# One float32 stream on SyncE's queue and one bf16 stream on GpSimd's, and the negated mean made by ScalarE, in a masked-patch loss kernel

## The chip, the cores and the metric

The kernel runs on one core of one Trainium2 chip. The metric is the device time of one execution in microseconds (us), as the median of several executions. A lower time is better.

## The reference

There are 32 images of 147 masked patches (75% of 196), each patch a row of 768 float32 numbers. `pred` and `target` both have the shape 32 x 147 x 768. Each row of the target is normalised by its own mean and variance, the squared distance to the predicted row is averaged over the row, and the row averages are averaged for each image:

```python
mean = target.mean(axis=-1, keepdims=True)
var = target.var(axis=-1, keepdims=True)
target = (target - mean) / np.sqrt(var + 1e-6)
loss = np.mean((pred - target) ** 2, axis=-1)
return loss.mean(axis=-1).astype(np.float32)
```

Both inputs together are 28.9 MB, all of which is read once; 32 numbers are written.

## The kernel before, in words

**Tiling.** Four partitions belong to each image, so 32 images fill 128 partitions. Each partition holds 37 rows of 768 numbers, called columns here and numbered 0 to 36; the last column of every fourth partition would lie outside the image, so the one with number 36 (called `REST`, line `REST = KM`) is loaded for 96 partitions alone. A column of 128 rows is 0.393 MB of float32 in memory. A "piece" is one DMA of up to four neighbouring columns, in which each partition receives one contiguous run (12 KB of source for four columns, 3 KB for one).

**Streams.** Pieces of the target are named t with their first column (t0, t4, ...), those of the prediction p. Before the change, t36 and t0 are loaded as float32 by SyncE's queue, and all 22 others by GpSimd's queue, which converts them to bf16 on the way. Their order is written out in the list `stream`: targets run about eight columns ahead of predictions, and it ends with t32-33, p24-27, t34-35, p28-29, p30-31, p32-33, p34, p35. At most eight pieces of GpSimd's queue are in flight: each issue from the ninth on waits on GpSimd for the landing of the piece eight places earlier.

**Stages of the work**, each by columns:

- `stats(g)` for a group g of columns: VectorE takes two `bn_stats` for each column (line 140) and one `bn_aggr` (line 141), which gives mean and variance (`mv`). Then, once for the group, ScalarE takes the square root of variance plus eps (line 142), VectorE takes the reciprocal `r` (line 143) and makes `nmr` = -mean * r (line 144). Groups have four columns, and two at the end.
- `normalise` on GpSimd (line 158): s = t * r + nmr for each column, written as bf16.
- `subtract` on TensorE (line 178) for a unit of two columns (one, for the last two units, 34 and 35, and for `REST`): three matmuls with minus the identity on s, then three with the identity on p, added up in a PSUM tile `z`. There are two `z` tiles, so a unit's first matmul waits until ScalarE has squared the unit two places earlier.
- `square` on ScalarE (line 184): z squared, summed along the row into a column of `rl`.
- `sums` on TensorE (line 190): a matmul with a mask adds up the four partitions of each image. At the end VectorE reduces 15 columns (line 224) and SyncE stores 32 numbers (line 225).

**Order.** Every engine works its own instructions strictly as they are listed. The list is made when the program is built: each step is given a due time by `at(when, step)` from simple planning costs and planned landings, and all steps are sorted by it. On ScalarE the small square roots of `stats` and the long squares stand in one sequence; likewise GpSimd holds both `normalise` and the issues of its DMAs. Near the end, ScalarE's sequence before the change is: square of unit 22 (columns 22 and 23), square of unit 24, square root of columns 34-35, then the squares of units 26, 28, 30, 32, 34 and 35.

Of the kernel before, what the change touches and what calls it, by code (L numbers as in the profile page):

```python
# [7 lines left out]
F32 = mybir.dt.float32  # L8
BF16 = mybir.dt.bfloat16
ALU = mybir.AluOpType  # L10
ACTF = mybir.ActivationFunctionType
# [3 lines left out]
def kernel(  # L15
# [19 lines left out]
    REST = KM  # L35
# [21 lines left out]
    for c in range(12, KM - 4, 4):  # L57
        stream += [("t", c, c + 4, "sw"), ("p", c - 8, c - 4, "sw")]
    stream += [("t", KM - 4, KM - 2, "sw"), ("p", KM - 12, KM - 8, "sw"), ("t", KM - 2, KM, "sw"),
               ("p", KM - 8, KM - 6, "sw"), ("p", KM - 6, KM - 4, "sw"), ("p", KM - 4, KM - 2, "sw"),  # L60
               ("p", KM - 2, KM - 1, "sw"), ("p", KM - 1, KM, "sw")]
# [7 lines left out]
    land, issue = {}, []  # L69
    t = 2.7  # L70
    for kind, c0, c1, q in stream:
        t += (c1 - c0) * D * 4 * rows_of(c0) / 430e3
        issue.append(t + 1.0)
        for c in range(c0, c1):
            land[kind, c] = t + 1.0
# [8 lines left out]
    def load(kind, c0, c1, q):  # L84
# [8 lines left out]
    lanes = [0.0] * 8  # L93
    k = 0
    for i, piece in enumerate(stream):
        if piece[3] == "hw":
            at(-1.0, lambda piece=piece: load(*piece))
        else:
            at(lanes[k % 8] + (0.01 * k), lambda piece=piece: load(*piece))
            lanes[k % 8] = issue[i] + 0.2  # L100
            k += 1

    ident = singles.tile([P, P], BF16)
    nident = singles.tile([P, P], BF16)
# [20 lines left out]
    def stats(g):  # L125
        n, K = rows_of(g[0]), len(g)
        r = small.tile([P, K], F32, name="r")
        nmr = small.tile([P, K], F32, name="nmr")
        for i, c in enumerate(g):
            rs[c] = (r[:n, i:i + 1], nmr[:n, i:i + 1])  # L130
        if not norm_pix_loss:
            pin(nc.vector.memset(r, 1.0))
            pin(nc.vector.memset(nmr, 0.0))
            return
        mv = small.tile([P, K, 2], F32, name="mv")
        for i, c in enumerate(g):
            til, o = tbuf[c]
            st = small.tile([P, 2, 6], F32, name="st")
            for j in range(2):
                pin(nc.vector.bn_stats(out=st[:n, j, :], in_=til[:n, o + j * half:o + (j + 1) * half]))  # L140
            pin(nc.vector.bn_aggr(out=mv[:n, i], in_=st[:n]))  # L141
        pin(nc.scalar.activation(out=r[:n], in_=mv[:n, :, 1], func=ACTF.Sqrt, bias=eps_t[:n], scale=1.0))  # L142
        pin(nc.vector.reciprocal(out=r[:n], in_=r[:n]))  # L143
        pin(nc.vector.scalar_tensor_tensor(out=nmr[:n], in0=mv[:n, :, 0], scalar=-1.0,  # L144
                                           in1=r[:n], op0=ALU.mult, op1=ALU.mult))


    def normalise(u, i):
        c = u[i]
        n = rows_of(c)  # L150
        if i == 0:
            s = work.tile([P, 2 * D], BF16, name="s")
            for m, cc in enumerate(u):
                sbuf[cc] = (s, m * D)
        s, so = sbuf[c]
        til, o = tbuf[c]
        r, nmr = rs[c]
# [36 lines left out]
    for g in groups:  # L194
        dve = max([dve] + [land["t", c] for c in g])
        at(dve, lambda g=g: stats(g))
        dve += 1.26 * len(g) + 0.8
        for c in g:
            u = next(u for u in units if c in u)
            pool = max(pool, dve + 0.1)  # L200
            at(pool, lambda u=u, i=u.index(c): normalise(u, i))
            pool += 1.1
            ready[c] = pool + 0.1
    free = [0.0, 0.0]
    for u in units:
# [7 lines left out]
        i = main_units.index(u) if u in main_units else -1  # L213
# [47 lines left out]
```

## Time and profile before

| what | value |
|---|---|
| median of 3 runs | 81.1 us (80.77 to 81.3) |
| the profiled execution: its time | 80.73 us |
| the profiled execution: its span, first to last instruction | 79.0 us |
| mean granted TensorE clock | 0.861 |
| busy time: TensorE matmuls, VectorE, ScalarE, GpSimd | 38.7, 45.7, 32.5, 50.1 us |
| `bn_stats` (line 140), one | 533 ns mean, 74 of them |
| `normalise` (line 158), one | 976 ns mean, 37 of them |
| square of two columns (line 184), one | 1431 ns mean, 17 of them |
| square root (line 142), one | 296 ns mean, 12 of them |
| `nmr` (line 144), one | 161 ns mean, 12 of them |
| issue of a target piece on GpSimd (line 89) | 589 ns mean, 9 of them |
| bytes written by DMA, packets | 15.43 MB, 3444 |
| bytes read from memory | 28.90 MB |

The page of a profile has numbered parts: busy times by engine; the span in 40 equal slices, with the busy share of each engine in tenths and the rate of the DMAs in GB/s; the DMA queues; the chain of work that ended last, followed back from the last instruction; and the costliest groups of instructions, with what ended the idle time before them. Beside the page, the trace answers questions: a timeline of instructions in a stretch of time, with the idle time before each and what released it, and the packets and bytes of each DMA queue in a stretch. `<-` in a group or timeline row stands between what is written and what is read. GB/s counts bytes as written, so a piece that is converted to bf16 counts half of what was read for it. One execution is profiled, so durations are of that one.

### The profile page before, as it was taken

Reading aid. Unit: us, or ns where it says so; the run is one execution under the profiler, and the core shown is the slowest. Engines: PE = TensorE matmul, PEld = TensorE weight load, DVE = VectorE, ACT = ScalarE, POOL = GpSimd, SP = SyncE. Lnnn points to the kernel's source line nnn. Section 1 sums busy time; section 2 is a strip of 40 time slices with the busy share of each in tenths; the row PEclk is TensorE's granted clock in tenths of the full one; section 3 lists DMA queues with packets and bytes.
Section 4 is the critical chain, followed back from the end, with each engine's and each line's share of the span. In section 5 each row is a group of like instructions: output and inputs, shape, how many; then the busy total and the mean of one; then the engine's idle time right before and its main releaser. Section 6 shows DMA issues by size and latency. Waiting matters only on the chain.

```text
span 79.0 us, 602 instructions
## 1 busy us (share of the span) xinstructions
PE 38.7 (49%) x126; PEld 13.4 (17%) x126; DVE 45.7 (58%) x137; ACT 32.5 (41%) x53; POOL 50.1 (63%) x73
## 2 busy tenths in 40 slices
PE   0000330008990069985317980991399496496500
PEld 0000210001320023231102320320131031223300
DVE  0061039979799799797797089529779267000000
ACT  5000000050100590872931760583134873999700
POOL 4998802059789899897797795399779360800000
PEclk9999999999999655599965569759956999999996
DMA  0799999999999999999999999999999999990000
GB/s 0 182 412 317 311 218 218 211 218 218 211 215 218 211 216 218 211 211 218 218 211 215 218 215 209 221 215 211 205 227 202 210 210 220 199 165 4 0 0 0
DMA packets 3444, 15.43 MB, mean 195 GB/s; under 512 B 432, under 2 KB 784, under 8 KB 3312
## 3 DMA queue, kind: packets, MB, share of 16 engines
q0 software_dynamic: 3136, 13.52, 84.2%
q1 hardware_dynamic: 304, 1.87, 6.2%
q14 instruction: 3, 0.02, 0.1%
q8 instruction: 1, 0.02, 0.1%
HBM read 28.90 MB, written 0.00 MB: 366 GB/s over the span
## 4 chain that ended last, share of the span: by engine, by line
DMA 42%; DVE 31%; ACT 7%; POOL 5%; PE 4%; issue 4%; SPq 1%; ACTq 0%
DMA p<-in_pred_dram 30%; DVE st L140 23%; DMA t<-in_target_dram 12%; DVE mv L141 5%; ACT z L184 5%; POOL s L158 5%; PE z L178 4%; ACT r L142 2%; DVE r L143 1%; DVE nmr L144 1%; SPq L89 1%; POOL t L89 1%; PE acc L190 0%; DVE ob L224 0%; ACTq L256 0%
## 5 line engine op out<-in xcount | busy, mean ns | idle before, releaser
L140 DVE BATCH_NORM_STATS2 st<-t 128x6 f32<-128x384 bf16 (+2 forms) x74 | 36.3, 533 | 14.4 <-DMA t<-in_target_dram 14.4
L158 POOL TENSOR_SCALAR s<-t,r,nmr 128x768 bf16<-128x768 bf16 (+2 forms) x37 | 35.9, 976 | 13.3 <-DVE nmr L144 13.0
L178 PE MATMUL z<-s,nident 128*128 128x512 bf16 (+3 forms) x57 | 21.4, 492 | 26.6 <-POOL s L158 23.7
L184 ACT ACTIVATE z<-z 128x1536 f32<-128x1536 f32 (+2 forms) x20 | 26.7, 1336 | 2.0 <-PE z L178 2.0
L178 PE MATMUL z<-p,ident 128*128 128x512 bf16 (+3 forms) x57 | 20.6, 478 | 8.9 <-DMA p<-in_pred_dram 8.9
L142 ACT ACTIVATE r<-mv,eps_t 128x4 f32<-128x4 f32 (+2 forms) x12 | 3.6, 296 | 39.4 <-DVE mv L141 39.4
L178 PEld LDWEIGHTS <-nident 128*128 128x128 bf16 (+1 forms) x57 | 5.8, 117 | 39.5 <-ACT z L184 16.3
L89 POOL DMA_DIRECT2D p<-in_pred_dram x13 | 7.7, 594 | 5.2 <-DMA t<-in_target_dram 3.2
L178 PEld LDWEIGHTS <-ident 128*128 128x128 bf16 (+1 forms) x57 | 7.0, 123 | 20.5 <-issue 17.8
L141 DVE BATCH_NORM_AGGREGATE mv<-st 128x2 f32<-128x12 f32 (+1 forms) x37 | 7.7, 208 | 1.3
L89 POOL DMA_DIRECT2D t<-in_target_dram x9 | 5.3, 589 | 0.0
L143 DVE RECIPROCAL r<-r 128x4 f32<-128x4 f32 (+2 forms) x12 | 2.1, 172 | 4.6 <-ACT r L142 4.6
L224 DVE TENSOR_REDUCE ob<-acc 32x1 f32<-32x15 f32 x1 | 0.2, 161 | 7.9 <-PE acc L190 7.9
L184 ACT ACTIVATION_READ_ACCUMULATOR z<-z 128x1 f32 (+1 forms) x20 | 3.7, 186 | 0.0
L144 DVE SCALAR_TENSOR_TENSOR nmr<-mv,r 128x4 f32<-128x4 f32 (+2 forms) x12 | 1.9, 161 | 0.4
L142 ACT ACT_TABLE_LOAD x1 | 1.3, 1283 | 0.8 <-PEq L242 0.8
L190 PE MATMUL acc<-rl,mask 128*32 128x1 f32 (+1 forms) x10 | 0.8, 179 | 0.8 <-ACT z L184 0.8
L190 PEld LDWEIGHTS acc<-rl,mask 128*32 128x32 f32 x10 | 0.5, 110 | 1.5 <-ACT z L184 0.9
L110 DVE MEMSET eps_t<- 128x1 f32 x1 | 0.1, 59 | 0.9 <-PEq L242 0.9
L112 POOL MEMSET ident<- 128x128 bf16 x1 | 0.4, 362 | 0.0
L113 POOL TENSOR_SCALAR_AFFINE_SELECT ident<-ident 128x128 bf16<-128x128 bf16 x1 | 0.3, 292 | 0.1
L113 POOL TENSOR_SCALAR_AFFINE_SELECT nident<-nident 128x128 bf16<-128x128 bf16 x1 | 0.3, 292 | 0.1
(13 smaller groups left out, 2.0 us busy)
## 6 DMA issues: line engine op xcount, KB each, us to landing
t<-in_target_dram POOLq DMA_DIRECT2D x7, 768.0 KB, 26.0
p<-in_pred_dram POOLq DMA_DIRECT2D x7, 768.0 KB, 26.6
t<-in_target_dram SPq DMA_DIRECT2D x1, 1536.0 KB, 9.7
p<-in_pred_dram POOLq DMA_DIRECT2D x3, 384.0 KB, 21.8
t<-in_target_dram POOLq DMA_DIRECT2D x2, 384.0 KB, 25.9
p<-in_pred_dram POOLq DMA_DIRECT2D x2, 192.0 KB, 16.4
t<-in_target_dram SPq DMA_DIRECT2D x1, 288.0 KB, 3.7
p<-in_pred_dram POOLq DMA_DIRECT2D x1, 144.0 KB, 3.7
```

What stands on the lines that cost most here:

```text
L89: pin(eng.dma_start(out=til[:n], in_=dram(x, c0, c1)))
L112: pin(nc.gpsimd.memset(til, 0.0))
L113: pin(nc.gpsimd.affine_select(out=til, in_=til, compare_op=ALU.not_equal, fill=v, base=0, pattern=[[-1, P]], channel_multiplier=1))
L140: pin(nc.vector.bn_stats(out=st[:n, j, :], in_=til[:n, o + j * half:o + (j + 1) * half]))
L141: pin(nc.vector.bn_aggr(out=mv[:n, i], in_=st[:n]))
L142: pin(nc.scalar.activation(out=r[:n], in_=mv[:n, :, 1], func=ACTF.Sqrt, bias=eps_t[:n], scale=1.0))
L143: pin(nc.vector.reciprocal(out=r[:n], in_=r[:n]))
L144: pin(nc.vector.scalar_tensor_tensor(out=nmr[:n], in0=mv[:n, :, 0], scalar=-1.0, in1=r[:n], op0=ALU.mult, op1=ALU.mult))
L158: pin(nc.gpsimd.tensor_scalar(out=s[:n, so:so + D], in0=til[:n, o:o + D], scalar1=r, scalar2=nmr, op0=ALU.mult, op1=ALU.add))
L178: pin(nc.tensor.matmul(z[:n, a:b], w[:n, :n], src[:n, so + a:so + b], start=first, stop=not first))
L184: pin(nc.scalar.activation(out=z[:n, :W], in_=z[:n, :W], func=ACTF.Square, accum_out=to))
L190: pin(nc.tensor.matmul(acc[:, 0:b - a], mask, rl[:, a:b], start=a == 0, stop=b == len(main_units)))
```

## The change

It does four things.

1. The whole target is now loaded as float32 by SyncE's queue, in ten DMAs in the order t0, t36, t4, t8, ... t32, all of four columns but t36. The ninth waits on SyncE for the landing of t0, the tenth for that of t36.
2. The whole prediction is loaded as bf16 by GpSimd's queue, in 13 DMAs: p0, p36, then p4 to p24 by fours, then p28, p30, p32 (two columns each), p34 and p35. Their due times start at `P_START` = 10.6, so on GpSimd's list the first stands behind the first `normalise` (which needs t0 and its statistics), and the next three behind one `normalise` each. Then p12, p16, p20 and p24 are issued together behind the fifth. The later ones wait for the piece eight places earlier.
3. The statistics of a group no longer make `nmr` on VectorE. ScalarE makes `nm` = -mean right behind the group's square root (new line 158), and `normalise` is now s = (t + nm) * r.
4. Groups and units are listed in another order: columns 0-1 and 2-3 are groups of their own and come ahead of `REST`, columns 28 to 31 are one group of four in place of two groups of two, and 32-33 and 34-35 stay groups of two. The planned landings that the due times rest on are worked out for two queues that share the rate equally.

Near the end, ScalarE's sequence is now (square root and `nm` of a group together): columns 28-31; squares of units 18 and 20; columns 32-33; square of unit 22; columns 34-35; squares of units 24, 26, 28, 30, 32, 34 and 35.

```diff
-    stream = [("t", REST, REST + 1, "hw"), ("t", 0, 4, "hw"), ("p", REST, REST + 1, "sw")]
-    stream += [("t", 4, 8, "sw"), ("t", 8, 12, "sw"), ("p", 0, 4, "sw")]
...
-    units = [(REST,)] + [(c, c + 1) for c in range(0, KM - 2, 2)] + [(KM - 2,), (KM - 1,)]
-
-    groups = [(REST,)] + [tuple(range(c, c + 4)) for c in range(0, KM - 8, 4)]
-    groups += [(c, c + 1) for c in range(KM - 8, KM, 2)]
...
+    t_pieces = [(0, 4), (REST, REST + 1)] + [(c, c + 4) for c in range(4, KM, 4)]
+    p_pieces = [(0, 4), (REST, REST + 1)] + [(c, c + 4) for c in range(4, 28, 4)]
+    p_pieces += [(28, 30), (30, 32), (32, 34), (34, 35), (35, 36)]
+
+    units = [(0, 1), (2, 3), (REST,)] + [(c, c + 1) for c in range(4, KM - 2, 2)] + [(KM - 2,), (KM - 1,)]
+
+    groups = [(0, 1), (2, 3), (REST,)] + [tuple(range(c, c + 4)) for c in range(4, KM - 4, 4)]
+    groups += [(KM - 4, KM - 3), (KM - 2, KM - 1)]
...
+    P_START = 10.6
...
-        til = data.tile([P, (c1 - c0) * D], F32 if q == "hw" else BF16, name=f"{kind}{c0}")
-        eng = nc.sync if q == "hw" else nc.gpsimd
+        til = data.tile([P, (c1 - c0) * D], F32 if kind == "t" else BF16, name=f"{kind}{c0}")
+        eng = nc.sync if kind == "t" else nc.gpsimd
...
+    for i, (c0, c1) in enumerate(t_pieces):
+        at(-1.0, lambda c0=c0, c1=c1: load("t", c0, c1))
+    for i, (c0, c1) in enumerate(p_pieces):
+        when = P_START + 1.5 * i
+        if i >= 8:
+            when = max(when, land["p", p_pieces[i - 8][0]] + 0.3)
+        at(when, lambda c0=c0, c1=c1: load("p", c0, c1))
...
+        pin(nc.scalar.activation(out=nm[:n], in_=mv[:n, :, 0], func=ACTF.Copy, scale=-1.0))
         pin(nc.vector.reciprocal(out=r[:n], in_=r[:n]))
-        pin(nc.vector.scalar_tensor_tensor(out=nmr[:n], in0=mv[:n, :, 0], scalar=-1.0,
-                                           in1=r[:n], op0=ALU.mult, op1=ALU.mult))
...
-        pin(nc.gpsimd.tensor_scalar(out=s[:n, so:so + D], in0=til[:n, o:o + D], scalar1=r, scalar2=nmr,
-                                    op0=ALU.mult, op1=ALU.add))
+        pin(nc.gpsimd.tensor_scalar(out=s[:n, so:so + D], in0=til[:n, o:o + D], scalar1=nm, scalar2=r,
+                                    op0=ALU.add, op1=ALU.mult))
```

More of the change, by code (lines that the diff above doesn't have):

```diff
@@ L52 @@
     psum1 = ctx.enter_context(tc.tile_pool(name="psum1", bufs=1, space=bass.MemoryType.PSUM))
-    stream = [("t", REST, REST + 1, "hw"), ("t", 0, 4, "hw"), ("p", REST, REST + 1, "sw")]
-    stream += [("t", 4, 8, "sw"), ("t", 8, 12, "sw"), ("p", 0, 4, "sw")]
[L57 to L61, printed above, removed]
@@ L63 @@
-    units = [(REST,)] + [(c, c + 1) for c in range(0, KM - 2, 2)] + [(KM - 2,), (KM - 1,)]
-    groups = [(REST,)] + [tuple(range(c, c + 4)) for c in range(0, KM - 8, 4)]
-    groups += [(c, c + 1) for c in range(KM - 8, KM, 2)]
[L69 to L75, printed above, removed]
+    t_pieces = [(0, 4), (REST, REST + 1)] + [(c, c + 4) for c in range(4, KM, 4)]
@@ new lines @@
+    p_pieces = [(0, 4), (REST, REST + 1)] + [(c, c + 4) for c in range(4, 28, 4)]
[4 more added lines that the diff above has]
+    P_START = 10.6
+    land = {}
+    jobs = {"t": [2.2, list(t_pieces)], "p": [P_START + 1.3, list(p_pieces)]}
@@ new lines @@
+    now = 0.0
+    left = {}
+    while jobs:
+        live = [q for q in jobs if jobs[q][0] <= now]
+        if not live:
+            now = min(j[0] for j in jobs.values())
+            continue
+        for q in live:
+            if q not in left:
+                c0, c1 = jobs[q][1][0]
+                left[q] = (c1 - c0) * D * 4 * rows_of(c0) / 432e3
+        step = min(left[q] for q in live) * len(live)
+        later = [jobs[q][0] - now for q in jobs if q not in live]
+        step = min([step] + later)
+        now += step
+        for q in live:
+            left[q] -= step / len(live)
+            if left[q] < 1e-9:
+                del left[q]
+                c0, c1 = jobs[q][1].pop(0)
+                for c in range(c0, c1):
+                    land[q, c] = now + 0.9
+                if not jobs[q][1]:
+                    del jobs[q]
@@ L82, with load @@
     tbuf, pbuf, sbuf, rs = {}, {}, {}, {}
-    def load(kind, c0, c1, q):
+    def load(kind, c0, c1):
         x = targ_f if kind == "t" else pred_f
         n = rows_of(c0)
-        til = data.tile([P, (c1 - c0) * D], F32 if q == "hw" else BF16, name=f"{kind}{c0}")
-        eng = nc.sync if q == "hw" else nc.gpsimd
+        til = data.tile([P, (c1 - c0) * D], F32 if kind == "t" else BF16, name=f"{kind}{c0}")
+        eng = nc.sync if kind == "t" else nc.gpsimd
         pin(eng.dma_start(out=til[:n], in_=dram(x, c0, c1)))
@@ L91, in load @@
             (tbuf if kind == "t" else pbuf)[c] = (til, (c - c0) * D)
[L93 to L101, printed above, removed]
+    for i, (c0, c1) in enumerate(t_pieces):
[5 more added lines that the diff above has]
+        at(when, lambda c0=c0, c1=c1: load("p", c0, c1))
     ident = singles.tile([P, P], BF16)
@@ L127, in stats @@
         r = small.tile([P, K], F32, name="r")
-        nmr = small.tile([P, K], F32, name="nmr")
+        nm = small.tile([P, K], F32, name="nm")
         for i, c in enumerate(g):
-            rs[c] = (r[:n, i:i + 1], nmr[:n, i:i + 1])
+            rs[c] = (r[:n, i:i + 1], nm[:n, i:i + 1])
         if not norm_pix_loss:
             pin(nc.vector.memset(r, 1.0))
-            pin(nc.vector.memset(nmr, 0.0))
+            pin(nc.vector.memset(nm, 0.0))
             return
@@ L156, in normalise @@
         til, o = tbuf[c]
-        r, nmr = rs[c]
-        pin(nc.gpsimd.tensor_scalar(out=s[:n, so:so + D], in0=til[:n, o:o + D], scalar1=r, scalar2=nmr,
-                                    op0=ALU.mult, op1=ALU.add))
+        r, nm = rs[c]
+        pin(nc.gpsimd.tensor_scalar(out=s[:n, so:so + D], in0=til[:n, o:o + D], scalar1=nm, scalar2=r,
+                                    op0=ALU.add, op1=ALU.mult))
     main_units = [u for u in units if u[0] != REST]
```

## The prediction

> **What bounds the kernel now.** I read the 40 slices of the page first.
>
> ```profile
> DMA  0799999999999999999999999999999999990000
> GB/s 0 182 412 317 311 218 218 211 218 218 211 215 218 211 216 218 211 211 218 218 211 215 218 215 209 221 215 211 205 227 202 210 210 220 199 165 4 0 0 0
> HBM read 28.90 MB, written 0.00 MB: 366 GB/s over the span
> ```
>
> The DMA engines are full from slice 1 to slice 35. Bytes count as written, so 215 GB/s of bf16 are 430 GB/s read. By 4.0 us, narrow windows show 0.30 MB float32 and 0.07 MB bf16 (0.14 read), so at about 420 GB/s the stream starts in effect at 2.95. The window 70.5 to 71.0 has 80 GB/s in place of 215, so it ends near 70.7: 28.9 MB in 67.75 us, 426.6 GB/s. The span ends 8.3 us later. What fills those 8 us is in the timeline of the tail.
>
> ```profile
> 63.24 1.43 ACT L184 ACTIVATE z<-z 128x1536 f32<-128x1536 f32 x1
> ...
> 63.97 1.02 DVE L140 BATCH_NORM_STATS2 st<-t 128x6 f32<-128x384 bf16 x2 [1.70 <-DMA t<-in_target_dram]
> ...
> 66.45 0.29 ACT L142 ACTIVATE r<-mv,eps_t 128x2 f32<-128x2 f32 x1 [1.66 <-DVE mv L141]
> 66.66 1.43 ACT L184 ACTIVATE z<-z 128x1536 f32<-128x1536 f32 x1
> ...
> 68.11 1.43 ACT L184 ACTIVATE z<-z 128x1536 f32<-128x1536 f32 x1
> 68.26 0.33 PEld L178 LDWEIGHTS <-nident 128*128 128x128 bf16 x3 [2.10 <-ACT z L184]
> ...
> 69.83 1.44 ACT L184 ACTIVATE z<-z 128x1536 f32<-128x1536 f32 x1 [0.17 <-PE z L178]
> ...
> 71.28 1.44 ACT L184 ACTIVATE z<-z 128x1536 f32<-128x1536 f32 x1
> ...
> 72.72 0.80 ACT L184 ACTIVATE z<-z 128x768 f32<-128x768 f32 x1
> ...
> 73.80 0.80 ACT L184 ACTIVATE z<-z 128x768 f32<-128x768 f32 x1 [0.16 <-PE z L178]
> ...
> 75.20 0.37 SPq L225 DMA_DIRECT2D out_dram<-ob  x1
> ```
>
> The reader is to see ScalarE wait. The last target piece lands, its statistics start at 63.97, and ScalarE stands 1.66 us at the square root of columns 34-35 until 66.45. Unit 26's square is behind it although its z is ready. Then a backlog of six squares runs until 74.6: ScalarE and TensorE take turns over two z tiles, so two squares take 3.17 us (66.66 to 69.83), not 2 x 1.43. The last square starts at 73.80, 9.83 us after the last target landed; p35 is long there. So the end is set by **when the last target has landed, and how many squares stand behind its square root**. The page's chain, "DMA p<-in_pred_dram 30%", does not tell this.
>
> The answer on DMA queues shows how they share from 6 to 10 us, while SyncE's t0 (12 KB runs) meets GpSimd's t4 (the same runs):
>
> ```profile
> q0 software_dynamic: 70, 0.43, 53.2%
> q1 hardware_dynamic: 67, 0.82, 49.7%
> ```
>
> The columns are packets, MB written and share of the engines' time. 67 packets against 70: 0.82 MB in 4 us is 206 GB/s of float32, and 0.43 MB of bf16 is 0.86 read, 215 GB/s. One packet each in turn, the software queue slightly ahead.
>
> **What the Trainium skill says.** "DMA: Bandwidth & Descriptors", section "Issuing engines are not separate DMA queues": all issuers end on the same 16 engines and interleave, so a second queue adds no bandwidth. The trace agrees: about 420 GB/s read with two queues (6 to 10 us), 430 with one. The same page, "Queues, rings and completion order": each engine takes turns between queues packet by packet; 67 to 70 agrees. "TensorE: Matmul & The Clock Gate", its first table: ScalarE's queue is strictly first in, first out; the square held at 66.45 agrees. The price of `nm` is on "ScalarE: Activation LUTs", "What ACT_TABLE_LOAD costs": 280 ns plus 0.83 per element with a pointer bias, 186 with immediates. The first agrees with the square root (295 ns), so I take 190 ns, issued 0.21 us after the square root as the next square is now (66.45 to 66.66). Bounds: 0.1 to 0.3 us.
>
> **The change part by part.**
>
> *VectorE.* 12 `nmr` of 161 ns go: -1.9 us of busy time. In the tail a group takes 2.48 us from landing to square root (63.97 to 66.45), and the next statistics follow 0.45 us after the square root's start (0.33 to the reciprocal, 0.17 long, overlapped; now 0.58, 58.50 to 59.11). Gain 0.1 us once on the path.
>
> *ScalarE.* 12 `nm`: about 0.2 us each, all hidden behind waits for DMA but the two of the last groups: +0.4 us. GpSimd gets both operands no later: `nm` ends 0.4 us after the square root starts, `r` 0.5; before, `nmr` 0.69. Should `nm` load another table each time (1.28 us in this trace), it would be 2.6 us on the path; the build holds one load, so I count nothing.
>
> *GpSimd.* Nine target issues of 589 ns go (5.3 us). The p issues that wait for an old piece have `normalise` behind them: p32 waits for p4 (30.8 below), p34 for p8 (37.9), p35 for p12 (45.1). Held are columns 10, 15 and 20 and what follows; TensorE needs them with p8, p12 and p20, each at least 7 us later, against 1 us a column. Nothing on the path; bare, up to 3 us each. bf16 or float32 input is alike: 977 and 974 ns for `normalise`, 532 for `bn_stats`. SyncE issues ten DMAs of 0.65 us; only the output stands behind them.
>
> *Transfers.* Bytes read do not change: 28.9 MB at 426.6 again ends at 70.7. What changes is the order.
> - t alone from 2.95 at 420 (mean of 449, 418 and 406 between 4.5 and 6.0). t0 lands at 2.95 + 3.75 + 1.1 = 7.8 (lag: t0's bytes end at 10.1 now, landing 11.24). Two columns' statistics, square root and one `normalise`: 7.8 + 2.48 + 0.55 + 0.98 = 11.8, where p0 is issued. p36's first packets came 1.7 us after its issue: p starts at 13.4. By then 10.45 x 0.42 = 4.39 MB of t are in, 10.06 remain.
> - Shared, t at 208 and p at 220 GB/s read: p0 until 20.5. p36 has 3 KB packets and takes 2 us, t about 0.6 MB in it (now t0 moves 0.34 MB between 4 and 5 us, beside p36). Then t has 10.06 - 1.49 - 0.6 = 7.97 MB, 38.3 us: **t ends at 60.85, and t32 with columns 32 to 35 lands at 61.6** (61.5 to 61.95 for a lag of 0.65 to 1.1).
> - p, landings: p4 30.8, p8 37.9, p12 45.1, p16 52.2, p20 59.4. Then alone: p24 about 63.5, p32 about 69, p35 about 71.8.
>
> *The tail.* t28 lands at 54.4, so the square root of columns 28-31 runs at 59.1, unit 18's square at 59.5, unit 20's at 61.0, done 62.4. VectorE takes columns 32-33 from 61.6: square root 64.1, `nm` 64.3, unit 22's square 64.5. Statistics of 34-35 start at 64.55, square root at 67.03, `nm` at 67.24, unit 24's square at **67.45**. Behind it stand seven squares, units 24 to 35, where six stood. With the rhythm of now (offsets 0, 1.45, 3.17, 4.62, 6.34, then 2.52 from the last double to the last start): 67.45 + 6.34 + 2.52 = **76.3**, against 73.80. All z inputs are there: unit 26's tile is freed at 66.0, p35 at 71.8 is needed at 75. So the end is 14.7 us after the last target's landing, not 9.83, and that landing is only 2.4 us earlier: **+2.5 us**. The terms: +2.93 a second group behind the last landing, +1.59 one square more, +0.4 `nm`, -0.1 `nmr`, makes +4.8; -2.4 for the landing.
>
> Sum against the profiled execution: span 79.0 + 2.5 = 81.5; around the span lie 80.73 - 79.0 = 1.73; time 83.2. The median of before stands 0.37 above that execution: **83.6, say 83.5**.
>
> **Rivals.**
> 1. *The target gets more than its half, and p20 binds.* Before columns 32-33's square root may run, all of t and p up to p20 must be in (unit 20's square stands ahead): 14.45 + 9.73 = 24.2 MB, 56.7 us, thus 59.65, lands 60.8 whoever is last. Then matmuls 0.82 to 1.49, square 1.45: square root at 63.2 to 63.8 in place of 64.1. Time 83.6 - 0.3 to 0.9: 82.7 to 83.3 in the median. For: 3 KB and two-column p packets lose turns. Against: 67 to 70.
> 2. *The target gets less, or TensorE is slow in the tail.* At 200 GB/s for t, 1.6 us later, nothing saved. Three cold matmuls take 1.49 us in place of 0.82 (57.39 to 60.31): 0.65 a unit in the two-tile rhythm, up to 2.6. Time 85 to 87. For: the granted clock is 0.69 in 50 to 60. Against: it was 0.95 to 1.0 in this same backlog.
> 3. *The backlog is gone; the transfer alone sets the end.* p35 at 71.8, last square at 72.4, -1.4 us: 79.7. Against: p24 to p35 land after 63, and ScalarE's list still has two stops.
> 4. *Faster, one mechanism: two queues carry more than one.* Place: the shared phase. The window 4 to 6 gives 0.75 + 0.16 read = 455 GB/s, which speaks for it; 6 to 10 gives 420, against. Each 1% brings the 24.2 MB in 0.57 us earlier. It ties at 446 GB/s and is over 1% faster from about 452.
> 5. *Same, the edit is hidden:* the last landing at 59 rather than 61.6 (a faster t-alone rate and an earlier start together), 80.5 to 81.9.
>
> **How the numbers follow.** The forecast of late landing 0.58 (its own range 82.8 to 84.6: half a microsecond for the t-alone rate, 0.4 for the lag, one for p's start and p36); rival 1 0.14; rival 2 0.13; rivals 3 and 4 together 0.06; rival 5 0.09. About 1%, 0.8 us, is what a measurement of this kernel can tell from no change. Slower 0.85, same 0.09, faster 0.06. The range 82.2 to 85.6 leaves out no more than two in ten: below, rival 5 and the faster ones; above, the far half of rival 2.
>
> **What would show it.** In the profile after: a GB/s row near 410 until slice 6, near 320 until about slice 30, then near 215; t32's first statistics near 61.6 and a wait for the target before it; ScalarE waiting at the last two square roots (64.1 and 67.0) with units 22 and 24 ready; seven squares after the last; the last square at 76.3. It is wrong if the last statistics begin before 59, if ScalarE's last wait is for z and not for `mv`, or if the shared phase is far from 320 GB/s.

## The result, and the profile after

The kernel before took 81.2 us in the median of four runs (80.77 to 81.44), the changed one **84.07 us** in the median of four (83.34 to 84.38). The ratio is 1.035, with a 95% interval of 1.027 to 1.043: slower, as forecast (83.5, range 82.2 to 85.6). The profiled execution of the changed kernel took 83.96 us, with a span of 82.3 and a granted clock of 0.856. Some executions of a kernel are slower than its others: the ratios leave these out, and where the profiled one is such an execution (84.76 us under "The list alone", 83.87 us with p planned at 6.6) its timeline is read only to about 1 us.

First the 40 slices, here the DMA row and the rate, and the bytes read.

```profile
DMA  0999999999999999999999999999999999900000
GB/s 0 275 442 329 400 418 436 376 332 314 308 364 396 313 318 311 326 320 320 311 317 332 323 314 314 320 324 281 209 221 206 203 212 209 167 4 0 0 0 0
HBM read 28.90 MB, written 0.00 MB: 351 GB/s over the span
```

A slice is 2.06 us here. The DMA engines are full from slice 1 to slice 34, until about 71, where they were before: the stream did not get longer. The row has the three levels that the prediction named: about 420 while the target runs alone, about 318 while the two streams share, about 210 (420 read) when the prediction runs alone. But the step from about 320 to about 210 comes in slice 27, near 57, and not near 61. **The target was read about 4 us earlier than forecast**.

Now the tail: the timeline of VectorE's, ScalarE's and TensorE's decisive rows. The columns are start, duration, engine and line, operation, `written<-read`, how many, and in brackets the idle time before it with what ended it. "PE L192 ... x3" is half of TensorE's work for a unit of two columns: three matmuls on s or three on p.

```profile
57.59 1.44 PE L192 MATMUL z<-p,ident 128*128 128x512 bf16 x3 [4.05 <-DMA p<-in_pred_dram]
...
58.82 1.49 PE L192 MATMUL z<-s,nident 128*128 128x512 bf16 x3
...
59.12 1.44 ACT L198 ACTIVATE z<-z 128x1536 f32<-128x1536 f32 x1 [4.72 <-PE z L192]
...
60.10 1.49 PE L192 MATMUL z<-p,ident 128*128 128x512 bf16 x3
...
60.56 0.29 ACT L157 ACTIVATE r<-mv,eps_t 128x4 f32<-128x4 f32 x1
...
60.88 0.18 DVE L159 RECIPROCAL r<-r 128x4 f32<-128x4 f32 x1 [3.30 <-ACT r L157]
...
60.98 0.99 DVE L155 BATCH_NORM_STATS2 st<-t 128x6 f32<-128x384 f32 x2
...
61.68 1.44 ACT L198 ACTIVATE z<-z 128x1536 f32<-128x1536 f32 x1 [0.74 <-PE z L192]
...
62.35 0.81 PE L192 MATMUL z<-p,ident 128*128 128x512 bf16 x3
...
63.26 1.44 ACT L198 ACTIVATE z<-z 128x1536 f32<-128x1536 f32 x1
...
64.70 0.28 ACT L157 ACTIVATE r<-mv,eps_t 128x2 f32<-128x2 f32 x1
...
65.02 0.17 DVE L159 RECIPROCAL r<-r 128x2 f32<-128x2 f32 x1 [1.68 <-ACT r L157]
...
67.56 0.29 ACT L157 ACTIVATE r<-mv,eps_t 128x2 f32<-128x2 f32 x1 [0.87 <-DVE mv L156]
...
67.86 1.43 ACT L198 ACTIVATE z<-z 128x1536 f32<-128x1536 f32 x1
...
76.71 0.80 ACT L198 ACTIVATE z<-z 128x768 f32<-128x768 f32 x1 [0.16 <-PE z L192]
...
78.11 0.37 SPq L239 DMA_DIRECT2D out_dram<-ob  x1
```

Read it from the top. At 57.59 p16 has landed; TensorE had waited 4.05 us for it. ScalarE squares unit 16 at 59.12, after 4.72 us of waiting for that z, and only then, at 60.56, takes the square root of columns 28-31, which stands behind it in the list. Those statistics had been ready since 57.6. VectorE stood still for 3.30 us, because its reciprocal needs that square root, and so the statistics of columns 32-33 begin at 60.98 **without any wait for the target**. The same thing in small comes at 64.70: the square root of columns 32-33 stands behind unit 20's square (63.26), VectorE waits 1.68 us. The last square root is at 67.56, and seven squares stand behind it, from 67.86 to the last start at 76.71 (before: six squares, 73.80).

A second thing is in these rows. The first matmuls behind the wait for p16 are slow: three take 1.44 to 1.49 us (57.59, 58.82, 60.10), where three take 0.81 later (62.35). The granted clock was 0.50 between 57.5 and 61.4. ScalarE waits for them: unit 18's square starts 0.74 us after ScalarE is free (61.68). The kernel before at the same time:

```profile
56.62 0.97 PE L178 MATMUL z<-p,ident 128*128 128x512 bf16 x3 [3.00 <-DMA p<-in_pred_dram]
...
57.39 1.49 PE L178 MATMUL z<-s,nident 128*128 128x512 bf16 x3
...
58.50 0.29 ACT L142 ACTIVATE r<-mv,eps_t 128x2 f32<-128x2 f32 x1 [2.79 <-DVE mv L141]
58.67 1.49 PE L178 MATMUL z<-p,ident 128*128 128x512 bf16 x3
...
58.70 1.43 ACT L184 ACTIVATE z<-z 128x1536 f32<-128x1536 f32 x1
```

It has p20 at 56.62, and squares unit 20 at 58.70. Its matmuls are as slow there (57.39, 58.67), but ScalarE is waiting for statistics at the time (58.50), so that they cost it nothing.

What that means in work is in the table of stretches. The columns are PE, PEld, DVE, ACT and POOL busy time (and instructions), the clock, the DMA share and GB/s. First the kernel before, its stretch from 70 us to the end:

```profile
70.00:82.00 12.00, 3.55 (x26) 1.56 (x24) 0.16 (x1) 4.54 (x8) 0.00 (x0) 0.86 0.07 13
```

and the changed kernel, the same stretch:

```profile
70.00:82.00 12.00, 6.00 (x36) 2.43 (x35) 0.16 (x1) 7.12 (x12) 0.20 (x1) 0.88 0.16 28
```

ScalarE has 7.12 us of work after 70.0 in place of 4.54. The 2.6 us more, in four more instructions, are the two units by which it is behind when the stream ends: in the kernel before it squared unit 20 at 58.70, in the changed one unit 16 at 59.12.

The answer on waits says the same over the whole kernel. ScalarE's squares waited 2.0 us in all for TensorE before, and 20.7 us now; TensorE waited 8.9 us for p before, and 23.7 us now. VectorE waited for the target once in the whole changed kernel, for t0.

### The profile page after: what moved, and what is told of

The parts are those of the page before. It is cut to its first block, busy times and chain, and to the rows that moved or that the text cites. A ratio compares the mean times of both kernels' runs of the same rounds, so it can differ in the third digit from the quotient of the medians.

```text
span 82.3 us, 611 instructions
## 1 busy us (share of the span) xinstructions
PE 35.8 (44%) x124; PEld 12.9 (16%) x126; DVE 43.1 (52%) x125; ACT 33.7 (41%) x65; POOL 45.1 (55%) x64
## 4 chain that ended last, share of the span: by engine, by line
DMA 56%; DVE 14%; PE 10%; ACT 9%; issue 5%; POOL 1%; ACTq 0%
DMA p<-in_pred_dram 47%; DVE st L155 11%; PE z L192 10%; DMA t<-in_target_dram 9%; ACT z L198 7%; DVE mv L156 2%; ACT r L157 1%; DVE r L159 1%; POOL p L106 1%; PE acc L204 0%; ACT nm L158 0%; DVE ob L238 0%; ACTq L270 0%; ACTq L198 0%; ACTq L157 0%
## 5 line engine op out<-in xcount | busy, mean ns | idle before, releaser
L172 POOL TENSOR_SCALAR s<-t,nm,r 128x768 bf16<-128x768 f32 (+1 forms) x37 | 35.9, 978 | 12.2 <-DVE r L159 10.5
L155 DVE BATCH_NORM_STATS2 st<-t 128x6 f32<-128x384 f32 (+1 forms) x74 | 36.1, 529 | 7.0 <-DMA t<-in_target_dram 7.0
L198 ACT ACTIVATE z<-z 128x1536 f32<-128x1536 f32 (+2 forms) x20 | 26.8, 1339 | 20.9 <-PE z L192 20.7
L192 PE MATMUL z<-p,ident 128*128 128x512 bf16 (+3 forms) x55 | 19.4, 468 | 23.7 <-DMA p<-in_pred_dram 23.7
L192 PE MATMUL z<-s,nident 128*128 128x512 bf16 (+3 forms) x57 | 19.9, 460 | 17.6 <-POOL s L172 13.2
L192 PEld LDWEIGHTS <-ident 128*128 128x128 bf16 (+1 forms) x57 | 6.5, 114 | 34.1 <-issue 30.6
L192 PEld LDWEIGHTS <-nident 128*128 128x128 bf16 (+1 forms) x57 | 5.8, 116 | 29.3 <-issue 16.6
L158 ACT ACTIVATE nm<-mv 128x4 f32<-128x4 f32 (+2 forms) x12 | 2.3, 189 | 0.0
```

What stands on the lines that cost most here:

```text
L158: pin(nc.scalar.activation(out=nm[:n], in_=mv[:n, :, 0], func=ACTF.Copy, scale=-1.0))
L192: pin(nc.tensor.matmul(z[:n, a:b], w[:n, :n], src[:n, so + a:so + b], start=first, stop=not first))
L198: pin(nc.scalar.activation(out=z[:n, :W], in_=z[:n, :W], func=ACTF.Square, accum_out=to))
```

## The experiments

Three theories at first. **A**: what sets the end is ScalarE's list, which holds a finished group's square root behind a square that waits for p16. **B**: the end follows p16's landing itself. **C**: as in the prediction, the end follows the last landing of the target. Later ones are named where they come in.

### The list alone

Only the planned landings of p are moved by 5 us, so that the list puts these square roots ahead of the squares; no transfer, operation or size changes.

```diff
-    jobs = {"t": [2.2, list(t_pieces)], "p": [P_START + 1.3, list(p_pieces)]}
+    jobs = {"t": [2.2, list(t_pieces)], "p": [P_START + 1.3 + 5.0, list(p_pieces)]}
```

> The changed kernel with p planned to start 5 us later, which is nearer to what its trace shows. The DMAs are the same and stand in the same order; only the lists of ScalarE, TensorE and GpSimd change, so that the square root of columns 28-31 stands ahead of the square of unit 14 and that of 32-33 ahead of unit 16. Theory A (ScalarE's list holds the statistics back while it waits for p16): the statistics of 32-33 start near 58 and not at 61.0, the wait for the last square root goes, and the last square starts at about 76.0 in place of 76.7; 0.5 to 1.5 us faster than the changed kernel. Theory B (the landing of p alone sets the end, whatever the list): no difference, within 0.3 us. Theory C (the prediction's own, the last target's landing sets the end): no difference.

Measured: 83.73 us (83.26 to 84.76), ratio to before 1.031 (1.026 to 1.036). From its timeline:

```profile
57.96 1.02 DVE L155 BATCH_NORM_STATS2 st<-t 128x6 f32<-128x384 f32 x2 [2.16 <-DMA t<-in_target_dram]
...
60.45 0.30 ACT L157 ACTIVATE r<-mv,eps_t 128x2 f32<-128x2 f32 x1 [3.30 <-DVE mv L156]
...
60.74 1.43 ACT L198 ACTIVATE z<-z 128x1536 f32<-128x1536 f32 x1
...
63.65 0.28 ACT L157 ACTIVATE r<-mv,eps_t 128x2 f32<-128x2 f32 x1
...
65.51 1.44 ACT L198 ACTIVATE z<-z 128x1536 f32<-128x1536 f32 x1 [1.48 <-PE z L192]
```

The hold is gone: VectorE now waits for the target itself (57.96), and the last square root comes at 63.65, 3.9 us earlier. Yet the time is only 0.3 us lower, with overlapping ranges. The square of unit 16 (60.74) now waits behind the square root of columns 32-33, 1.6 us later than in the changed kernel, and unit 20 waits 1.48 us for TensorE, whose six matmuls took about 1.47 us a three there. The list decides which of the two waits ScalarE takes. Theory A, as a gain to be had by freeing the statistics, is not confirmed: the squares that are still to come set the end just as much. Nor is it ruled out, since the slow matmuls are in the way here too: by an estimate, at 0.81 us a three unit 20's square would have waited next to nothing of its 1.48 us.

### p16 earlier, by moving p36

p36 and its unit are moved behind p24, so that every p piece up to p24 lands earlier.

```diff
-    p_pieces = [(0, 4), (REST, REST + 1)] + [(c, c + 4) for c in range(4, 28, 4)]
-    p_pieces += [(28, 30), (30, 32), (32, 34), (34, 35), (35, 36)]
...
+    p_pieces = [(c, c + 4) for c in range(0, 28, 4)]
+    p_pieces += [(REST, REST + 1), (28, 30), (30, 32), (32, 34), (34, 35), (35, 36)]
...
```

> The changed kernel with p36, the piece of 3 KB packets, moved from second place of p's queue to behind p24, and unit REST with it. Theory B (p16 lands 5 us late, of which about 2.6 us are p36's small packets taking turns with the target's large ones, and the end follows it): p16 lands near 54 in place of 57.5 and the end comes 2 to 3.5 us earlier. Theory A (the list decides): in the list that this plan gives, units 16 and 18 stand ahead of the square root of 28-31 and units 20 and 22 ahead of that of 32-33, so that the last square root is near 67.8 as now with a unit more behind it: the end is within 1.2 us of the changed kernel, later rather than earlier. Both: without p36 in the shared phase the target ends about 3 us later, near 60.

Measured: 88.27 us, ratio 1.086 (1.080 to 1.093). A second kernel keeps this and plans p 3 us later, so that only its list differs:

> e2 (p36 behind p24) with p planned to start 3 us later. The DMAs stay as in e2; ScalarE's list has the square root of 28-31 ahead of units 16 and 18 and that of 32-33 ahead of units 20 and 22. Theory A (in e2 the square roots stood behind squares that wait for p20, and the last one came at 69.1): the last square root comes at about 66, the last square at 77 to 78 in place of 80.7, 2.5 to 3.7 us faster than e2. If the list has nothing to do with it: as e2, 88.3 us.

Measured: 85.51 us, ratio 1.058 (1.051 to 1.066). The tail of the first of the two:

```profile
53.23 0.81 PE L192 MATMUL z<-p,ident 128*128 128x512 bf16 x3 [2.54 <-DMA p<-in_pred_dram]
...
65.95 0.28 ACT L157 ACTIVATE r<-mv,eps_t 128x2 f32<-128x2 f32 x1
...
69.12 0.29 ACT L157 ACTIVATE r<-mv,eps_t 128x2 f32<-128x2 f32 x1 [2.79 <-DVE mv L156]
```

p16 is there at 53.23, 4.4 us earlier than in the changed kernel, and the kernel is 4.2 us slower. Theory B falls, and theory A's number for this kernel (within 1.2 us of the changed one) is missed too. t32 had landed by 60.43, but the list has the squares of units 20 and 22 (62.02 and 64.51) ahead of the square root of columns 32-33 at 65.95; the last one follows at 69.12, with 11.6 us to the last square (80.68), in which the unit of column 36 now stands too and ScalarE waits 1.55 us for slow matmuls before unit 28's square. With the other list that last square root is at 66.07, the last square at 78.75, and the time 2.8 us lower. So here the list is worth 2.8 us with the transfers unchanged, where in the changed kernel another list was worth nothing that can be told.

### The shared phase earlier

p's issue is planned at 3.0, so p0 is issued at 3.08, ahead of any `normalise`.

```diff
-    P_START = 10.6
+    P_START = 3.0
```

> The changed kernel with P_START 3.0 in place of 10.6: GpSimd issues p0 behind its constants, near 3.2 us, while no normalise runs, and SyncE's queue is already full. If the 4.0 us from p0's issue to its first packet come from the queue of the target being ahead in the engines, the delay is 3 us or more here too; if they come from GpSimd being busy with normalise, it is about 1.7 us as in the kernel before. Theory C (the last landing of the target sets the end): the target lands at 66 to 68 and the end comes 9.8 us after it for the start of the last square, 76 to 78, thus between 1 us faster and 1.3 us slower than the changed kernel. Theory B: p16 lands some 7 us earlier and the end comes 3 us or more earlier.

Measured: 82.87 us (82.77 to 82.89), ratio 1.022 (1.020 to 1.025). The last target landing is a wait again:

```profile
65.86 1.02 DVE L155 BATCH_NORM_STATS2 st<-t 128x6 f32<-128x384 f32 x2 [0.88 <-DMA t<-in_target_dram]
...
71.21 0.29 ACT L157 ACTIVATE r<-mv,eps_t 128x2 f32<-128x2 f32 x1 [0.37 <-DVE mv L156]
...
75.54 0.80 ACT L198 ACTIVATE z<-z 128x768 f32<-128x768 f32 x1 [0.16 <-PE z L192]
```

Two groups behind the landing take 5.35 us, and four squares are left: the last starts 9.7 us after the landing, as theory C has it for this order. The landing is about 8 us later than in the changed kernel, and the time is 1.2 us **lower**. The two streams balance: what the target gains, the prediction loses.

Issued earlier still (`P_START = 0.5`, p0 at 1.32):

> The changed kernel with P_START 0.5: p0 is issued ahead of GpSimd's constants, at 0.8 us together with SyncE's first target piece; the others follow from 3 us as in e3. First packets: if the 3.8 us of e3 are the target's packets that are queued ahead of p0, the delay is below 2.5 us here, with almost nothing queued. The end, by theory C (the target's last landing, 9.7 us to the start of the last square): p0 takes 1.6 MB of transfers from the lone target at the start, so the target lands 0.5 to 2 us later than in e3 and the end is that much later, 83.3 to 85 us. If p alone decides: faster than e3.

Measured: 84.54 us, ratio 1.044 (1.037 to 1.050). The last target landing is at 67.00, the last square root at 72.37, the last square at 77.27, 10.3 us after the landing. So the best of these starts lies between 1.3 and 12 us. A theory **D** put it where both streams are equally late, with p's issue in between: GpSimd is kept busy to 7.6 by 12 small operations on a spare tile, and p planned at 6.6; p0 is issued at 7.56.

> The changed kernel with p0 issued at about 6.6 us, between e3 (3.1) and the changed kernel (12.0): GpSimd does a memset and twelve affine selects on a spare tile first, which nothing reads, and P_START is 6.6. Theory D (the end is a balance: the earlier p starts, the later the last target and its square roots, the later p starts, the more squares are left when it lands; both e9 and the changed kernel lie on the slopes): the first p packet near 10.5, the target lands near 62 to 63, p20 near 58, and the end lies below both neighbours, 81.3 to 82.5 us. Rival (p's start matters in one direction only, earlier is better down to e3): 82.9 to 84.1 us, between the two.

Measured: 83.19 us (82.31 to 83.87), ratio 1.022 (1.018 to 1.026), the same as with 3.0. p16 was there at 53.23 and p20 at 60.60, the target's last bytes at about 61. But ScalarE's list had the square root of columns 28-31 behind a square that waits for p again, unit 20's this time (62.13, then 63.57), the last square root was at 71.96 and the last square at 76.22. The two streams came as close together as intended, and the gain did not come: theory D falls as far as this list goes. Whether another list would bring it was not tried.

### The last target piece in halves

Starting from the kernel with `P_START = 3.0`, the last target piece is cut into two of two columns, so that columns 32-33 land before 34-35.

```diff
-    t_pieces = [(0, 4), (REST, REST + 1)] + [(c, c + 4) for c in range(4, KM, 4)]
+    t_pieces = [(0, 4), (REST, REST + 1)] + [(c, c + 4) for c in range(4, 32, 4)] + [(32, 34), (34, 36)]
```

> The changed kernel with p issued from 3 us (as in e3) and the last target piece of four columns cut into two pieces of two. In e3 the target lands last (65.9), and the end follows it: two groups' statistics, then four squares, last square at 75.5. Theory C in this form (with p early, the last landing of the target sets the end): columns 34-35 still land near 65.9, but only one group's statistics come after; the last square root is near 68.4 in place of 71.2, the list has one square more behind it, and the last square starts at 74.0 to 74.8: 0.7 to 1.5 us faster than e3, level with the kernel before within 1%. If the landing is not what binds in e3: as e3 within 0.3 us.

Measured: 84.82 us, ratio 1.049 (1.042 to 1.056): slower, a miss. The queues between 60 and 62 us, first with the piece whole, then with it in halves; q1 is SyncE's queue with the target, q0 GpSimd's with the prediction (packets, MB written, share of the engines' time):

```profile
q1 hardware_dynamic: 47, 0.58, 68.9%
q0 software_dynamic: 44, 0.11, 28.5%
```

```profile
q1 hardware_dynamic: 72, 0.44, 54.9%
q0 software_dynamic: 69, 0.18, 44.2%
```

Packets take turns in both (47 to 44, 72 to 69), but the target's are 12 KB in the first and 6 KB in the second. With half the size the target gets 0.44 MB in place of 0.58, its last landing comes at 68.35 in place of 65.86, and one square more stands behind the last square root. The two outweigh the earlier start of a group: the last square starts at 76.81 in place of 75.54.

### nmr and nm

Part 3 undone in the changed kernel, and part 3 alone in the kernel before. The edit of the first, without the one in `normalise` that goes with it:

```diff
-        pin(nc.scalar.activation(out=nm[:n], in_=mv[:n, :, 0], func=ACTF.Copy, scale=-1.0))
...
+        pin(nc.vector.scalar_tensor_tensor(out=nm[:n], in0=mv[:n, :, 0], scalar=-1.0,
+                                           in1=r[:n], op0=ALU.mult, op1=ALU.mult))
...
```

> The changed kernel with the old form of the statistics: VectorE makes -mean * r behind the reciprocal and ScalarE makes no negated mean. All theories: within 0.4 us of the changed kernel. By the sum, three nm of 0.19 us go from ScalarE's path in the tail and two nmr of 0.16 us come to VectorE's: 0.2 to 0.3 us faster. Rival (moving the mean to ScalarE was worth having): 0.5 us slower or more.

> The kernel before with part 3 of the change alone: ScalarE makes the negated mean, VectorE no nmr, normalise adds and multiplies. Every theory: within 0.4 us of the kernel before; by the sum, one nm of 0.19 us joins ScalarE's path ahead of the last six squares and nothing is won, so 0.1 to 0.2 us slower.

Measured: 84.13 us, ratio 1.036 (1.030 to 1.041), and 81.18 us, ratio 0.999 (0.997 to 1.002). Part 3 is worth nothing that can be told, in either kernel.

### Where the 4 us of the target came from

p0 was issued at 12.00, yet its first packet is just before 16.0, about 3.9 us later, where I had taken 1.7 us from p36 of the kernel before. Theory **E**: they queue behind the target packets that the engines have already in hand, and packets of half the size would halve the delay. Target columns 4 to 15 are cut into pieces of two.

```diff
-    t_pieces = [(0, 4), (REST, REST + 1)] + [(c, c + 4) for c in range(4, KM, 4)]
+    t_pieces = [(0, 4), (REST, REST + 1)] + [(c, c + 2) for c in range(4, 16, 2)] + [(c, c + 4) for c in range(16, KM, 4)]
```

> The changed kernel with target columns 4 to 15 in pieces of two columns, so that the target's packets are 6 KB and not 12 KB while p0 is issued and p36 moves; p is as in the changed kernel. Theory E (a new queue's first packet waits for about eight packets of the other queue in each engine, whatever their size: 8 x 16 x 12.3 KB at 0.42 MB per us is 3.75 us, measured 4.0, 3.8 and 4.3; before, six of 3 KB and two of 12 KB give 1.64, measured 1.7): the delay from p0's issue is 2.0 to 2.4 us in place of 4.0. Rival (a busy queue costs a fixed time): 4 us. By equal turns p0 then moves at two thirds of the rate and p36 at one third, so p16 lands near 52 in place of 57.6 and the target near 61; the end 0.5 to 1.5 us earlier than in the changed kernel.

Measured: 84.03 us, ratio 1.035 (1.030 to 1.039). p0 was issued at 11.85, the first packets came between 15.5 and 16.0: 3.7 us or a little more. E falls, and the time is that of the changed kernel, not 0.5 to 1.5 us less. Theories **F** (the delay grows with the size of the first p DMA) and **G** (it belongs to starting one queue while the other runs at the full rate) were told apart by p36 ahead of p0, and by p0 in halves.

```diff
-    p_pieces = [(0, 4), (REST, REST + 1)] + [(c, c + 4) for c in range(4, 28, 4)]
+    p_pieces = [(REST, REST + 1), (0, 4)] + [(c, c + 4) for c in range(4, 28, 4)]
```

> The changed kernel with p36 (3 KB packets, 144 KB written) issued ahead of p0 and nothing else changed; the whole result is still computed. It asks why the second queue's first packets came 4.0 us after their issue at 12.0, where p36 in the kernel before needed 1.7. Theory G (the delay belongs to starting a queue while the other one runs at full rate): first p packets still 3.5 to 4.2 us after the issue. Theory F (the delay grows with the size of the DMA that is issued; p36 is a quarter row per partition, p0 is four): first p packets 1.7 to 2.5 us after the issue, about 14. In time both say little: under G within 0.5 us of the changed kernel's 84.07; under F the shared phase starts up to 2 us earlier, p16 lands about 1 us earlier and the time is 83.0 to 84.0.

> The changed kernel with p0 issued as two DMAs of two columns each (6 KB packets), one DMA more in all; the whole result is still computed. Theory G: first p packets 3.5 to 4.2 us after the issue at 12.0, as with one p0 of four columns. Theory F: about 2.3 to 3.2 us, between p36's 1.7 and p0's 4.0. In time: within 0.7 us of the changed kernel's 84.07 under both; the 6 KB packets of p0 take equal turns against the target's 12 KB ones, which gives the target more for about 4 us, and that alone should move p16's landing by some 2 us at most, later.

Measured: 83.61 us, ratio 1.028 (1.022 to 1.034), and 84.50 us, ratio 1.040 (1.036 to 1.043). In the first, p36 was issued at 11.41; this is the window from 15.0 to 15.5, where its first packets are:

```profile
q1 hardware_dynamic: 22, 0.15, 70.5%
q0 software_dynamic: 9, 0.01, 15.1%
```

That is 3.6 to 4.1 us for a DMA with 3 KB packets. In the second, 12.01 to between 15.5 and 16.0. F falls, and of the three theories G is left. Read in windows of 0.1 us, the delay is 3.7 to 4.1 us in the eleven kernels that issue their first p piece between about 3 and 12 us, whatever the size of the DMA (144 to 768 KB written), of its packets (3, 6, 12 KB) or of the target's (6 or 12 KB). But p0 issued at 1.32, when SyncE's queue was itself just starting with t0, needed 4.4 us, while p36 issued at 1.36 in the kernel before, where SyncE's queue starts with t36 and its 3 KB packets, needed 1.9 to 2.0. G does not explain these two. What sets the delay stays open.

These three kernels gave a test that was not planned for: they shift the target against the prediction with ScalarE's list unchanged (but for one early square in the last of them, long before the tail). First the one with the target in small pieces, then the one with p0 in halves.

```profile
54.16 1.44 PE L192 MATMUL z<-p,ident 128*128 128x512 bf16 x3 [4.10 <-DMA p<-in_pred_dram]
...
62.66 1.02 DVE L155 BATCH_NORM_STATS2 st<-t 128x6 f32<-128x384 f32 x2 [2.12 <-DMA t<-in_target_dram]
...
68.02 0.30 ACT L157 ACTIVATE r<-mv,eps_t 128x2 f32<-128x2 f32 x1 [0.85 <-DVE mv L156]
```

```profile
67.63 0.29 ACT L157 ACTIVATE r<-mv,eps_t 128x2 f32<-128x2 f32 x1 [0.73 <-DVE mv L156]
...
76.77 0.80 ACT L198 ACTIVATE z<-z 128x768 f32<-128x768 f32 x1 [0.16 <-PE z L192]
```

| kernel | target's last bytes | p16 there | last square root | last square |
|---|---|---|---|---|
| target in small pieces | about 61, landing 62.66 | 54.16 | 68.02 | 77.17 |
| changed kernel | about 57 | 57.59 | 67.56 | 76.71 |
| p36 first | about 57 | 56.85 | 66.94 | 76.08 |
| p0 in halves | about 53.5 | by 58.29 | 67.63 | 76.77 |

The target ends over a range of some 7 us, and the last square over one of 1.1 us. In the first row the last square starts 14.5 us after the last target landing: that is the prediction's picture, 14.7 us, almost to the letter. In the other three VectorE does not wait for the target in the tail at all: ScalarE's list holds the square root of columns 28-31 behind unit 16's square, which waits for p16, or, with p0 in halves, that of columns 24-27 behind unit 12's, for which p12 came at 54.01 (50.22 in the changed kernel).

## Why the prediction was right, and which step of it failed

**What bounds the kernel: right.** The stream ends near 71 in both kernels, and the tail behind it decides.

**Bytes and the end of the stream: right.** 28.9 MB ended at about 71 with two queues as with one; the shared phase ran at 214 GB/s of target and 212 read for the prediction (30 to 40 us), against my 208 and 220. The section "Issuing engines are not separate DMA queues" of the Trainium skill's page "DMA: Bandwidth & Descriptors" says as much; these numbers agree, and rival 4 falls.

```profile
q1 hardware_dynamic: 190, 2.14, 51.7%
q0 software_dynamic: 188, 1.06, 51.1%
```

**The step that failed: "t ends at 60.85, and t32 with columns 32 to 35 lands at 61.6".** The bytes were in at about 57, and p16, which the same sums put at 52.2, landed at 57.59. Two terms of the sum were mis-sized. p's start: "p36's first packets came 1.7 us after its issue: p starts at 13.4"; it was about 3.9 us and 16.0, which left the target alone for 2.6 us more, about 0.55 MB gained over its half. And p36: "takes 2 us, t about 0.6 MB in it"; it took about 4 us, near 22.5 to 26.5. The window from 22 to 26 of the changed kernel:

```profile
q1 hardware_dynamic: 117, 1.28, 77.0%
q0 software_dynamic: 107, 0.21, 27.8%
```

Turns are still equal (117 to 107), but p36's packets are a quarter of the target's in bytes, and the target gets 77% of the engines' time. I had taken the rate beside p36 from a moment of the kernel before when the queues had only begun. The direction was that of my rival 1 (the target gets more than its half), the size larger: the wait went from the target to p16, not to p20.

**The tail: right in size, in part by luck.** The landing that the forecast made the cause came some 4 us early, and a hold that it did not have stood in its place, within 0.6 us of the time. From the forecast to the trace:

- Statistics of columns 32-33: forecast 61.6 by the landing; measured 60.98, by the release of VectorE. -0.6.
- The square root of columns 32-33 to the last one: I had it wait for its own statistics alone. In the trace it stands behind unit 20's square, and VectorE waits 1.68 us. So the last square root is 6.58 us after those statistics begin, not 5.43: +1.15.
- `nm` and the start of unit 24's square: 0.30 us behind the square root, not 0.42: -0.12.
- Unit 24's square: forecast 67.45, measured 67.86. The sum of the three is +0.4.
- Seven squares behind it: forecast 8.86 us to the last start, measured 8.85 (67.86 to 76.71). So 76.71 against 76.3.
- From the last square to the end of the span: 5.6 us, where the kernel before had 5.2: +0.4.

That makes the span 82.3 for 81.5, and the time 83.96 for 83.2 on the same basis. The release at 60.98 is a cause that the forecast did not have: the prediction had the square root of columns 28-31 at 59.1, waiting for nothing but its statistics, and it came at 60.56 behind unit 16's square. Of the signs that the prediction named, the three rates and the seven squares are there; the wait for the target before t32's statistics is not, nor ScalarE's wait at the first of the last two square roots. Where the target's landing did bind, with the target in small pieces, the forecast's picture held (14.5 us for 14.7).

**Why slower at all.** The rate of the stream is that of before, and so is its end. Before, targets and predictions alternate in one order, target about eight columns ahead, and at 56.62 TensorE had p20. The changed kernel has read all of the target by then, and p16 comes at 57.59. At that time ScalarE is two units behind, and a unit takes 1.6 us in the rhythm of two z tiles: two times 1.6 us is 3.2, and the last square is 2.9 us later. That arithmetic is an argument, and the slow matmuls behind p16's wait are a rival to it: an estimate from the tail's rows, with 0.81 us for each three, brings unit 16's square 0.6 us and the squares and square roots behind it up to 1.6 us earlier. Every timeline of this case has such slow matmuls after 50 us, so how the 2.9 us divide between p's lateness and TensorE's pace is not shown. What the runs show is this. Between the four kernels of the table the target's end moves by 7 us with p moving the other way, and the last square by no more than 1.1 us: an early target, paid for with a late p16 or p12, earned nothing. And taking p earlier at the target's expense (`P_START` 3.0) gives 1.2 us back.

**The other steps.** t0 landed at 7.97 (7.8), p0 was issued at 12.00 (11.8): right. `nm` 189 ns (190), one table load in the profile: right; and part 3 is nothing by two runs, so the +0.4 and -0.1 us that I gave it were hidden or too small to tell. GpSimd's issues: p's waits for earlier pieces were 12.0 us of its time, over five waits, the longest 4.1 (I had up to 3 us bare); TensorE waited for `normalise` only twice, both times before 14 us, so these waits are not seen on the path, though no run took them away by themselves. Rival 5 had the edit hidden if the last landing came at 59; it came before 58, and nothing was hidden, so the landing was not the lever that I took it for. Rival 3 fell with the trace, which shows the backlog. Of rival 2, a slow TensorE, a part came true: the last seven squares kept the rhythm of before (8.85 us), but ahead of them three matmuls took the 1.49 us that it had named, on ScalarE's path.

No version of the changed kernel that was run comes below the kernel before. The best, with `P_START` 3.0, is 2.2% above it.

## What to carry to other kernels

When two streams feed one product, bytes that arrive before they can be used are paid for by the bytes that the other stream did not get; lay out who is needed when, and compare which unit of work the last engine has reached at a fixed time, not how early either stream ends. In an engine that works its list strictly in order, a short instruction that releases another engine should stand ahead of a long one that waits for data, but putting it there moves the long one: look at what is left in the backlog before hoping for a gain. Equal turns between queues are equal packets, so the piece with the smaller rows gets the smaller share.

## What the runs showed of the hardware that I had not expected

- GpSimd's queue, started while SyncE's ran, had its first packets 3.7 to 4.1 us after the issue in eleven kernels, whatever the sizes of DMA and packets. Started together with SyncE's it needed 4.4 us in one kernel, and 1.9 to 2.0 us for p36 in the kernel before. The cause is open.
- Turns are by packet, and a row's packet counts as one, 3 KB or 12 KB: 117 to 107 packets gave the target 77% of the engines' time, and 190 to 188 equal packets gave 52%. The Trainium skill's page "DMA: Bandwidth & Descriptors", section "Queues, rings and completion order", has the turns by packet; that the shares then go by the packets' size is what these windows add.
- `bn_stats` and `normalise` took the same time on float32 as on bf16 input (529 and 978 ns here, 533 and 976 before), so the wider target cost these engines nothing.
